# Attention times values with the values stationary: two 64-column halves of the array, one head in each

## The chip, the cores and the metric

The kernel runs on one core of one Trainium2 chip. The metric is the device time of one execution in microseconds (us). TensorE (PE) multiplies matrices; its weight loads are listed apart as PEld. VectorE (DVE), ScalarE (ACT) and GpSimd (POOL) work on elements; SyncE (SP) issues most DMAs. Every engine works through its own instructions strictly in the order in which they were written down.

## The reference

One decoder layer over 256 tokens of width 1024. The token mixer has three groups (a gated recurrence, a gated linear attention of 4 heads, and causal softmax attention of 8 heads of width 64), whose outputs go side by side through one output projection; a squared-ReLU MLP follows. With 256 tokens there is one key block, so the attention group is plain causal attention with a linear position bias:

```python
s_own = jnp.einsum('bhqd,bhld->bhql', q_blk, k_own) * scale
s_own = jnp.where(rel >= 0, s_own - slopes[:, None, None] * rel, NEG)
p = jax.nn.softmax(scores, axis=-1)
out = jnp.einsum('bhql,bhld->bhqd', p_own, v_own)
...
y = jnp.concatenate([rms_norm(ya, lru_out_norm), yb, rms_norm(yc, att_out_norm)], axis=-1)
x = x + jnp.einsum('bse,ed->bsd', y, w_out)
```

The attention output `yc` (256 tokens x 512 channels) is normalised over its 512 channels and multiplied by a gain per channel before the output projection.

## The kernel before, in words

Large products run as three matmuls (`mm3`, L299): every float32 operand is split into a high part of type float32r (an ACT copy, L71) and a low part (a DVE subtraction, L72), and high x high, high x low and low x high are added up. The small products of the three groups run in plain float32; the trace shows each of these matmuls as two records, one for each pass, so `x4` stands for two matmuls (a transpose has one record).

Weights come in chunks of 128x2048; chunk 0 to 11 are the input projection, 12 to 15 the output projection (two rows of 128 channels each), the rest is the MLP. `split_w` (in the plan `S_`, L96) splits half a chunk, and the second half also issues the load of the chunk three further on.

PE's order is written out: `slots` (L821) is the list of the quarters of the input projection (slots 8 to 47: twelve matmuls of 256 columns each), then the output projection (from slot 48: one channel block `k`, one quarter of the output, three matmuls of 512 columns each). Slots 48 to 63 take channel blocks 0 to 3, slots 64 to 67 channel blocks 4 to 7 of the first output quarter, and so on. The table `plan` (L826) names the steps that are issued ahead of each slot. A step puts its instructions into the queues of whichever engines it uses. So the table sets the order on all engines.

Of attention, each head `h` goes through: `at_mm` (scores for two heads; the two heads stand on different 64-row halves of the array, and each writes a PSUM bank of its own, L641), `at_max` (DVE, L646), `at_exp` (ACT with row sums, L653 and L654), `at_tr` (three PE transposes of the 128x384 probabilities, L659), `at_pt` (ACT copies the result to SBUF, L663). Then for four heads at a time: `at_av` multiplies with the values. There the transposed probabilities are stationary (128 columns to load) and 64 value columns stream (L674 to L676), so the output has tokens on partitions. `at_norm` (DVE, L683 and L684) divides by the row sums, `at_sq` (ACT, L691) makes sums of squares, `at_rms` and `at_scale` (DVE and POOL, L696, L152, L701) apply the norm per token. `at_out_tr` transposes the result with eight PE transposes (L168), since the output projection wants channels on partitions, and `at_out_split` (L175, L176) applies the gain and splits into `yTh` and `yTl`.

PSUM has eight banks; `mis` takes the one that has been idle longest, `free` gives it back.

Of the kernel before, what the change touches and what calls it, by code (L numbers as in the profile page):

```python
# [11 lines left out]
AF = mybir.ActivationFunctionType  # L12
OP = mybir.AluOpType
AX = mybir.AxisListType

P = 128
# [12 lines left out]
SP_LAM, SP_LB, SP_LN, SP_AN, SP_WA, SP_WX, SP_N = 30, 32, 34, 36, 40, 296, 552  # L29
# [3 lines left out]
def trunk_kernel(ctx: ExitStack, tc, x, x_t, w_in, w_out, w_ff1, w_ff2, small, hg_norm, norm_final, out):  # L33
    nc = tc.nc
    V, A, G, T = nc.vector, nc.scalar, nc.gpsimd, nc.tensor
# [12 lines left out]
    def mis(name):  # L48
        b = idle.pop(0)
        held[name] = (b,)  # L50
        return banks[:, b, :]
# [55 lines left out]
    sp = xa[:, 0:SP_WA]  # L107
# [33 lines left out]
    ident = const.tile([P, P], F32, name="ident")  # L141
# [23 lines left out]
    def transposes(pair, src, k0, t):  # L165
        for n in range(4):
            i = n // 2
            T.transpose(pair[n % 2][:, i * 256 + t * 128:i * 256 + (t + 1) * 128],  # L168
                        src[:, t, (k0 + n) * P:(k0 + n + 1) * P], ident)

    def evac_split(pair, gain, oh, ol, k0, ns=range(4)):
        for n in ns:
            k = k0 + n
            ps = pair[n % 2][:, (n // 2) * 256:(n // 2 + 1) * 256]
            A.activation(oh[:, k, :], ps, AF.Copy, scale=gain[:, k:k + 1])  # L175
            V.scalar_tensor_tensor(ol[:, k, :], ps, gain[:, k:k + 1],  # L176
                                   oh[:, k, :].bitcast(F32), op0=OP.mult, op1=OP.subtract)

    ones = const.tile([P, 64], F32, name="ones")
# [150 lines left out]
    yTh = wt("yTh", [P, KT, S], dt=F32R)  # L330
    yTl = wt("yTl", [P, KT, S], dt=F32R)
# [7 lines left out]
    att_d = wt("att_d", [P, 8, 128])  # L339
# [126 lines left out]
    rr = {}  # L466
# [33 lines left out]
    su = wt("su", [P, 512])  # L500
# [111 lines left out]
    cq = [wt(f"cq{g}", [P, 2, 256], tag=("cq0", "xb_y")[g]) for g in range(2)]  # L612
    ck = [wt(f"ck{g}", [P, 2, 256]) for g in range(2)]
    cv = wt("cv", [P, 2, 512])
    oc = wt("oc", [P, 2, 512])
    rsum = wt("rsum", [P, 2, 8])
    ps_s, sc_t, nm_t, pr_t, ps_t, PT = {}, {}, {}, {}, {}, {}

# [42 lines left out]
    def at_pt(h):  # L661
        PT[h] = wt("PT", [P, 384], tag="PT", bufs=8)
        A.copy(PT[h], ps_t[h][:, 0:384])  # L663
        free(f"pt{h}")

    ps_o = {}

    def at_av(g):
        ps = ps_o[g] = mis(f"av{g}")
        o = ps.rearrange("p (t h e) -> p t h e", t=2, h=4)  # L670
        for r in range(4):
            h = 4 * g + r
            vs = slice(h * 64, h * 64 + 64)
            T.matmul(o[:, 0, r, :], PT[h][:, 0:128], cv[:, 0, vs], start=True, stop=True)  # L674
            T.matmul(o[:, 1, r, :], PT[h][:, 128:256], cv[:, 0, vs], start=True, stop=False)  # L675
            T.matmul(o[:, 1, r, :], PT[h][:, 256:384], cv[:, 1, vs], start=False, stop=True)  # L676

    css = wt("css", [P, 2, 2])
    csq = wt("csq", [P, 2, 256], tag="su")

    def at_norm(g):
        ri = wt("ri", [P, 2, 4], tag="ri", bufs=2)
        V.reciprocal(ri, rsum[:, :, 4 * g:4 * g + 4])  # L683
        V.tensor_tensor(oc[:, :, g * 256:(g + 1) * 256].rearrange("p t (h e) -> p t h e", e=64),  # L684
                        ps_o[g].rearrange("p (t h e) -> p t h e", t=2, h=4),
                        ri[:, :, :, None].to_broadcast([P, 2, 4, 64]), op=OP.mult)
        free(f"av{g}")

    def at_sq(g):
        for t in range(2):  # L690
            A.activation(csq[:, t, :], oc[:, t, g * 256:(g + 1) * 256], AF.Square,  # L691
                         accum_out=css[:, g, t:t + 1])

    def at_rms():
        c2 = wt("c2", [P, 2])
        V.tensor_tensor(c2, css[:, 0, :], css[:, 1, :], op=OP.add)  # L696
        rr["c"] = rms_scale(c2, 512, 2, "cr")

    def at_scale():
        for t in range(2):  # L700
            V.tensor_scalar(oc[:, t, :], oc[:, t, :], rr["c"][:, t:t + 1], None, op0=OP.mult)  # L701

    oT = {}

    def at_out_tr():
        oT[0] = [mis(f"oT{b}") for b in range(2)]
        for t in range(2):
            transposes(oT[0], oc, 0, t)

    def at_out_split():  # L710
        evac_split(oT[0], sp[:, SP_AN:SP_AN + 4], yTh[:, 4:8, :], yTl[:, 4:8, :], 0)
        free("oT0")
        free("oT1")


    tn = [(0, 0), (1, 0), (0, 1), (1, 1)]
# [95 lines left out]
    def x1_ss():  # L812
        for t in range(2):
# [6 lines left out]
    S_ = split_w  # L820
# [39 lines left out]
        33: [(hg_pred, 16), (at_mm, 0), (hg_mm, 32)],  # L860
        34: [(lr_ss,), (at_max, 0), (S_, 10, 1), (hg_pred, 32), (at_q, 1)],
        35: [(hg_up, 32)],
        36: [(lr_rms,), (at_max, 1), (at_exp, 0), (S_, 12, 0), (at_tr, 0), (at_k, 1)],
        37: [(hg_mm, 64), (at_mm, 1), (lr_bc,), (lr_rl,)],
        38: [
            (at_max, 2), (at_bias, 3), (at_pt, 0), (hg_pred, 64), (hg_up, 64), (at_exp, 1), (at_mm, 2),
            (at_bias, 4), (at_max, 3), (at_tr, 1), (at_max, 4), (lr_norm,), (hg_mm, 128), (at_exp, 2),
        ],
        39: [(at_bias, 5), (at_exp, 3), (at_tr, 2), (at_pt, 1), (at_max, 5), (S_, 11, 0)],
        40: [(at_mm, 3), (at_bias, 6), (hg_cross,), (hg_v,), (at_exp, 4), (at_max, 6)],  # L870
        41: [(at_bias, 7), (hg_av,), (at_tr, 3), (at_tr, 4), (at_max, 7)],
        42: [(at_pt, 2), (at_pt, 3), (S_, 12, 1)],
        43: [(at_exp, 5), (at_exp, 6), (S_, 11, 1), (hg_sq,), (hg_rms,)],
        44: [(at_pt, 4), (at_tr, 5), (at_v, 0), (S_, 13, 0), (at_exp, 7)],
        46: [(at_av, 0), (at_tr, 7), (at_norm, 0), (hg_out,), (at_pt, 7)],
        47: [(at_tr, 6), (at_pt, 5), (at_sq, 0)],
        48: [(x_load,), (lr_split,), (at_pt, 6)],
        50: [(hg_tr,), (S_, 13, 1)],
        51: [(at_v, 1), (at_av, 1), (at_norm, 1), (at_sq, 1)],
        52: [(at_rms,), (hg_split,)],  # L880
        54: [(at_scale,)],
        55: [(S_, 14, 0)],
        57: [(at_out_tr,)],
        58: [(S_, 14, 1)],
        63: [(S_, 15, 0), (at_out_split,)],
        64: [(S_, 15, 1), (S_, 16, 0)],
        68: [(S_, 16, 1)],
        72: [(x1_add, 0, 0), (x1_add, 1, 0)],
        77: [(x1_tr, 0, 0), (x1_tr, 0, 1)],
# [173 lines left out]
```

## Time and profile before

| what | value |
|---|---|
| median of 3 runs | 318.41 us (317.84 to 319.43) |
| profiled execution | 317.64 us, of which span 315.9 us |
| granted TensorE clock | 0.997 of full |
| PE busy | 307.5 us, 97% |
| DVE, ACT, POOL busy | 204.5, 173.6, 36.4 us |

The span runs from the first to the last instruction; 1.74 us of the profiled execution lie outside it. Matmuls are pipelined, so the duration of one record is longer than the time that it takes from its engine. The chain of waits cuts the span into pieces that follow one another; where PE is never idle, a piece of that chain is what an instruction costs PE.

### The profile page before, as it was taken

How to read it: one execution, taken by the hardware profiler on the slowest of the kernel's cores; microseconds unless marked ns; L12 is line 12 of the kernel's file. 1: busy time of each engine (PE TensorE's matmuls, PEld its weight loads, DVE VectorE, ACT ScalarE, POOL GpSimd, SP SyncE). 2: the span in 40 equal slices, each digit the busy share in tenths (PEclk: the TensorE clock that was granted, in tenths of full speed). 3: DMA queues.
4: the chain of work that ended last, by engine and by line, in shares of the span. 5: the costliest groups of instructions: out<-in, count | busy, mean ns of one | idle time of the engine just before them, and what ended most of it. 6: DMA issues, size and time to landing. Idle time of an engine off the chain costs nothing.

```text
span 315.9 us, 4816 instructions
## 1 busy us (share of the span) xinstructions
PE 307.5 (97%) x1908; PEld 270.7 (86%) x1908; DVE 204.5 (65%) x317; ACT 173.6 (55%) x297; POOL 36.4 (12%) x83
## 2 busy tenths in 40 slices
PE   8999999999999999999999999999999999999991
PEld 7999999998999888888888888888888888888881
DVE  1848999984545494686867745845754674575573
ACT  4769699684585370676635633552662463355241
POOL 8338900021401000000000000000000000000000
PEclk9999999999999999999999999999999999999998
DMA  7996553361036337038674366257336536621003
GB/s 198 411 399 231 189 214 133 135 226 41 2 135 266 134 134 268 0 133 334 261 270 166 110 257 228 92 214 264 118 151 266 164 114 256 233 102 65 0 9 126
DMA packets 9959, 55.68 MB, mean 176 GB/s; under 512 B 1232, under 2 KB 1488, under 8 KB 4048
## 3 DMA queue, kind: packets, MB, share of 16 engines
q1 hardware_dynamic: 9216, 54.06, 45.9%
q10 hardware_dynamic: 720, 1.31, 1.3%
q8 instruction: 15, 0.25, 0.3%
q14 instruction: 8, 0.07, 0.1%
HBM read 54.32 MB, written 1.05 MB: 175 GB/s over the span
## 4 chain that ended last, share of the span: by engine, by line
PE 93%; DMA 2%; issue 2%; DVE 1%; ACT 1%; POOLq 0%; POOL 0%; ACTq 0%; DVEq 0%
PE banks L770 19%; PE banks L301 19%; PE banks L302 18%; PE banks L303 18%; PE banks L771 10%; PE banks L405 2%; DMA raw<-in_w_in_dram 2%; PE banks L641 1%; PE banks L659 1%; PE banks L168 1%; PE banks L676 1%; PE banks L675 1%; PE banks L458 1%; PE banks L521 1%; PE banks L674 1%
## 5 line engine op out<-in xcount | busy, mean ns | idle before, releaser
L72 DVE TENSOR_TENSOR wl<-raw,wh 128x1024 fp32r<-128x1024 f32 (+1 forms) x100 | 113.6, 1183 | 21.5 <-ACT wh L71 21.5
L71 ACT CAST wh<-raw 128x1024 fp32r<-128x1024 f32 (+1 forms) x100 | 95.5, 1010 | 3.6 <-DMA raw<-in_w_in_dram 3.6
L770 PE MATMUL banks<-x1c,wh 128*128 128x512 f32 x256 | 90.9, 397 | 0.0
L771 PE MATMUL banks<-x1c,wl 128*128 128x256 f32 x256 | 71.8, 281 | 0.0
L770 PEld LDWEIGHTS banks<-x1c,wh 128*128 128x128 f32 x256 | 48.0, 188 | 11.7 <-DVE x1c L176 0.2
L302 PE MATMUL banks<-wl,uh 128*128 128x512 f32 (+1 forms) x132 | 51.4, 389 | 0.0
L303 PE MATMUL banks<-wh,ul 128*128 128x512 f32 (+1 forms) x132 | 51.4, 389 | 0.0
L301 PE MATMUL banks<-wh,uh 128*128 128x512 f32 (+1 forms) x132 | 51.4, 389 | 0.0
L771 PEld LDWEIGHTS banks<-x1c,wl 128*128 128x128 f32 x256 | 48.3, 189 | 0.7
L782 ACT COPY fb<-banks 128x256 f32<-128x256 f32 x32 | 11.8, 371 | 62.5 <-PE banks L771 62.5
L784 DVE TENSOR_TENSOR fs<-banks,fb 128x256 f32<-128x256 f32 x32 | 13.3, 423 | 42.9 <-ACT fb L782 42.9
L301 PE MATMUL banks<-hT,wh 128*128 128x256 f32 x128 | 37.5, 293 | 0.0
L302 PE MATMUL banks<-hT,wh 128*128 128x256 f32 x128 | 36.4, 284 | 0.5 <-DVE hT L162 0.5
L303 PE MATMUL banks<-hT,wl 128*128 128x256 f32 x128 | 36.3, 283 | 0.0
L303 PEld LDWEIGHTS banks<-wh,ul 128*128 128x128 f32 x132 | 24.8, 188 | 5.8 <-DVE ul L788 0.2
L301 PEld LDWEIGHTS banks<-wh,uh 128*128 128x128 f32 x132 | 24.8, 188 | 5.7
L302 PEld LDWEIGHTS banks<-wl,uh 128*128 128x128 f32 x132 | 24.9, 188 | 5.1
L302 PEld LDWEIGHTS banks<-hT,wh 128*128 128x128 f32 x128 | 24.5, 191 | 1.0 <-DVE hT L162 0.9
L301 PEld LDWEIGHTS banks<-hT,wh 128*128 128x128 f32 x128 | 24.6, 192 | 0.5
L303 PEld LDWEIGHTS banks<-hT,wl 128*128 128x128 f32 x128 | 24.5, 191 | 0.1
L969 POOL TENSOR_TENSOR r<-v,nhalf 128x1 f32<-128x1 f32 x2 | 1.1, 550 | 200.3 <-DVE v L965 200.3
L787 ACT CAST uh<-fu 128x512 fp32r<-128x512 f32 x16 | 9.9, 620 | 22.6 <-DVE fu L786 22.6
(197 smaller groups left out, 416.3 us busy)
## 6 DMA issues: line engine op xcount, KB each, us to landing
raw<-in_w_ff_dram SPq DMA_DIRECT2D x32, 1024.0 KB, 4.9
raw<-in_w_in_dram SPq DMA_DIRECT2D x10, 1024.0 KB, 5.9
raw<-in_w_out_dram SPq DMA_DIRECT2D x4, 1024.0 KB, 4.8
raw<-in_w_in_dram ACTq DMA_DIRECT2D x4, 256.0 KB, 7.2
xtok<-in_x_dram SPq DMA_DIRECT2D x2, 512.0 KB, 7.9
xa<-in_x_dram SPq DMA_DIRECT2D x2, 512.0 KB, 6.1
xa<-in_x_t_dram SPq DMA_DIRECT2D x3, 256.0 KB, 6.5
raw<-in_w_in_dram SPq DMA_DIRECT2D x2, 256.0 KB, 8.2
```

What stands on the lines that cost most here:

```text
L71: A.copy(hi, src)
L72: V.tensor_tensor(lo, src, hi.bitcast(F32), op=OP.subtract)
L168: T.transpose(pair[n % 2][:, i * 256 + t * 128:i * 256 + (t + 1) * 128], src[:, t, (k0 + n) * P:(k0 + n + 1) * P], ident)
L301: T.matmul(o, lh, rh, start=first, stop=False)
L302: T.matmul(o, lh, rl, start=False, stop=False)
L303: T.matmul(o, ll, rh, start=False, stop=last)
L405: T.matmul(ps[:, par, g * 64:(g + 1) * 64], kB[r, hp, hs], rhs, start=True, stop=True)
L770: T.matmul(o, wh[:, k, cs], flat(x1c[:, k]), start=k == 0, stop=False)
L771: T.matmul(o[:, 0:S], wl[:, k, cs], x1h[:, k, :], start=False, stop=k == KT - 1)
L782: A.copy(b[:, c, :], ff1_ps[j, c][:, S:])
L784: V.tensor_tensor(s_[:, c, :], ff1_ps[j, c][:, 0:S], b[:, c, :], op=OP.add)
L787: A.copy(uh[j], u)
```

## The change

The product with the values is turned round. The values of a head (64 columns) are stationary, and the transposed probabilities stream (256 columns for the first key block, 128 for the second). Two heads are paired: the output of the even one goes to partitions 0 to 63 of a bank, that of the odd one to partitions 64 to 127 of the same bank. The result has channels on partitions, as the output projection wants it, and the eight transposes of `oc` are gone. Since tokens now lie along the free axis, the division by the row sums is done ahead of the transposes, on the probabilities (`at_nrm`, DVE). The norm over channels is summed by a matmul with ones (`at_ss`), spread to all partitions by a matmul (`at_bc`), and applied together with the gain (`at_y`). The plan table is reordered from slot 36 to slot 68.

```diff
+    def at_nrm(h):
+        ri, pr = wt("ri", [P, 2], tag="ri", bufs=2), pr_t[h]
+        V.reciprocal(ri, rsum[:, :, h])
+        for t, s_ in enumerate((slice(0, 128), slice(128, 384))):
+            V.tensor_scalar(pr[:, s_], pr[:, s_], ri[:, t:t + 1], None, op0=OP.mult)
...
-    def at_av(g):
-        ps = ps_o[g] = mis(f"av{g}")
...
-            T.matmul(o[:, 0, r, :], PT[h][:, 0:128], cv[:, 0, vs], start=True, stop=True)
-            T.matmul(o[:, 1, r, :], PT[h][:, 128:256], cv[:, 0, vs], start=True, stop=False)
-            T.matmul(o[:, 1, r, :], PT[h][:, 256:384], cv[:, 1, vs], start=False, stop=True)
+    def at_av(c):
+        if c % 2 == 0:
+            av = mis(f"av{c // 2}")
+            ps_o[c], ps_o[c + 1] = av[:, 0:256], av[:, 256:512]
+        o = ps_o[c]
+        for kb, qs, ps in ((0, slice(0, 256), slice(0, 256)), (1, slice(128, 256), slice(256, 384))):
+            for par in range(2):
+                h = 2 * c + par
+                T.matmul(o[par * 64:(par + 1) * 64, qs], cv[:, kb, h * 64:(h + 1) * 64], PT[h][:, ps],
+                         start=kb == 0, stop=kb == 1)
...
+    def at_sq(c):
+        A.activation(osq_c[:, c, :], ps_o[c], AF.Square)
+    def at_sum(c, d):
+        V.tensor_tensor(osq_c[:, c, :], osq_c[:, c, :], osq_c[:, d, :], op=OP.add)
+    def at_ss():
+        ps_o["s"] = mis("ass")
         for t in range(2):
+            T.matmul(ps_o["s"][:, t * 64:(t + 1) * 64], osq_c[:, 0, t * 128:(t + 1) * 128], ones,
+                     start=True, stop=True)
     def at_rms():
+        rr["c"] = rms_scale(ps_o["s"].rearrange("p (t e) -> p t e", e=64)[:, 0:2, 0], 512, 2, "cr")
+        free("ass")
+    def at_bc():
+        ps_o["b"] = mis("RCps")
         for t in range(2):
-            V.tensor_scalar(oc[:, t, :], oc[:, t, :], rr["c"][:, t:t + 1], None, op0=OP.mult)
...
-            transposes(oT[0], oc, 0, t)
...
+            T.matmul(ps_o["b"][:, t * 128:(t + 1) * 128], rr["c"][:, t:t + 1].to_broadcast([P, P]), ident,
+                     start=True, stop=True)
+    def at_rl():
+        A.copy(RC, ps_o["b"][:, 0:256])
+        free("RCps")
+    def at_y(c):
+        V.scalar_tensor_tensor(yc[:, c, :], ps_o[c], sp[:, SP_AN + c:SP_AN + c + 1], RC,
+                               op0=OP.mult, op1=OP.mult)
+        if c % 2:
+            free(f"av{c // 2}")
+    def at_split(g):
+        ks = slice(4 + 2 * g, 6 + 2 * g)
+        split(flat(yTh[:, ks, :]), flat(yTl[:, ks, :]), flat(yc[:, 2 * g:2 * g + 2, :]))
...
-        46: [(at_av, 0), (at_tr, 7), (at_norm, 0), (hg_out,), (at_pt, 7)],
+        46: [(at_av, 0), (at_av, 1), (at_tr, 7), (hg_out,), (at_sq, 0), (at_sq, 1), (at_pt, 7)],
```

Three places show what the table moves. On PE, at slot 38, stand the scores of the third pair of heads (L641 before, L640 now), the transposes of head 1 (L659) and a product of the linear attention that also uses 64-row halves (L396). Before and now:

```order
-L641 MATMUL banks<-ck_199,cq_197 128x128 x2
-L641 MATMUL banks<-ck_199,cq_197 128x256 x2
-L659 MATMUL banks<-ident,pr 128x128 x3
+L640 MATMUL banks<-ck_199,cq_197 128x128 x2
+L640 MATMUL banks<-ck_199,cq_197 128x256 x2
 L396 MATMUL banks<-qd,kB 128x128 x4
```

The transposes no longer stand between the two products with 64-row halves; they come one slot later, alone.

On PE, at slot 46, before: the product with the values of heads 0 to 3 (four times three rows), then the transposes of head 7 and slot 46 itself.

```order
L303 MATMUL banks<-wh_1097,hT 128x256
L674 MATMUL banks<-cv,PT 128x64
L675 MATMUL banks<-cv,PT 128x64
L676 MATMUL banks<-cv,PT 128x64
...
L659 MATMUL banks<-ident,pr 128x128 x3
L301 MATMUL banks<-wh_1097,hT 128x256
```

The same place now:

```order
L303 MATMUL banks<-wh_1106,hT 128x256
L681 MATMUL banks<-PT,cv 64x256 x2
L681 MATMUL banks<-PT,cv 64x128 x2
...
L658 MATMUL banks<-ident,pr 128x128 x3
L301 MATMUL banks<-wh_1106,hT 128x256
```

Twelve matmuls of 64 streamed columns became eight matmuls on 64-column halves, four of 256 and four of 128 streamed columns; the second group of heads has the same rows at slot 50.

On DVE, from slot 50 on (`wl_1262` and `wl_1372` are the low parts of the output projection's chunks 13 and 14, `wl_1433` that of chunk 15), now:

```order
L72 TENSOR_TENSOR wl_1262<-raw_945,wh_1261 128x1024
L72 TENSOR_TENSOR wl_1372<-raw_1229,wh_1371 128x1024
L692 TENSOR_TENSOR osq_c<-osq_c 128x256 x2
L72 TENSOR_TENSOR yTl<-banks,yTh 128x512
L72 TENSOR_TENSOR wl_1372<-raw_1229,wh_1371 128x1024
L151 TENSOR_SCALAR crv<-banks 128x2
L715 SCALAR_TENSOR_TENSOR yc<-banks,xa,RC 128x256 x2
L72 TENSOR_TENSOR yTl<-yc,yTh 128x512
L715 SCALAR_TENSOR_TENSOR yc<-banks,xa,RC 128x256 x2
L72 TENSOR_TENSOR yTl<-yc,yTh 128x512
L72 TENSOR_TENSOR wl_1433<-raw_1203,wh_1432 128x1024 x2
```

Both halves of chunk 14 now stand ahead of the norm (`crv`), where before they stood behind it, and the whole tail of attention stands ahead of chunk 15.

## Rows read from the trace of the kernel before

**Rows 1.** The page: busy times, and the chain that ended last by engine.
```profile
PE 307.5 (97%) x1908; PEld 270.7 (86%) x1908; DVE 204.5 (65%) x317; ACT 173.6 (55%) x297; POOL 36.4 (12%) x83
...
PE 93%; DMA 2%; issue 2%; DVE 1%; ACT 1%; POOLq 0%; POOL 0%; ACTq 0%; DVEq 0%
```

**Rows 2.** Waits of PE's weight loads, 60 to 140 us: total, times, longest.
```profile
PEld banks L594 <- issue: 0.3, 1, 0.3
```

**Rows 3.** Busy time by engine in the attention stage (us, then busy and count).
```profile
69.50:101.90 32.40, 32.40 (x286) 30.71 (x285) 15.46 (x43) 19.52 (x57) 7.96 (x7) 1.00 0.33 127
```

**Rows 4.** Chain of waits, 94 to 113 us: start, length (us), what.
```profile
95.74 0.17 PE banks L674 x2
...
98.36 0.33 PE banks L659 x3
...
104.42 0.17 PE banks L674 x2
...
107.05 0.28 PE banks L301
107.33 0.23 PE banks L302
...
111.21 0.87 PE banks L168 x8
```

**Rows 5.** Chain of waits, 73 to 84 us.
```profile
74.31 0.71 PE banks L641 x8
...
77.94 0.48 PE banks L659 x3
...
80.69 0.33 PE banks L659 x3
...
82.45 0.86 PE banks L641 x8
83.31 0.31 PE banks L301
83.62 0.12 PE banks L302
```

**Rows 6.** Chain of waits, 67 to 69 us.
```profile
68.18 0.39 PE banks L584 x4
68.58 0.17 PE banks L301
```

**Rows 7.** Chain of waits, 21.5 to 24 us.
```profile
22.41 0.45 PE banks L232 x4
```

**Rows 8.** Chain of waits, 44 to 49 us.
```profile
45.09 0.86 PE banks L521 x4
```

**Rows 9.** The page's costliest groups: a weight load of the input projection.
```profile
L302 PEld LDWEIGHTS banks<-hT,wh 128*128 128x128 f32 x128 | 24.5, 191 | 1.0 <-DVE hT L162 0.9
```

**Rows 10.** DVE by line and shape, 75 to 116 us (busy, mean ns).
```profile
L72 DVE TENSOR_TENSOR wl<-raw,wh 128x1024 fp32r<-128x1024 f32 x8 | 9.6, 1223 | 5.8 <-ACT wh L71 5.8
...
L701 DVE TENSOR_SCALAR oc<-oc,crr 128x512 f32<-128x512 f32 x2 | 0.9, 485 | 0.0
L605 DVE SCALAR_TENSOR_TENSOR ya<-ya,xa,RL 128x256 f32<-128x256 f32 x2 | 0.9, 478 | 0.0
...
L151 DVE TENSOR_SCALAR crv<-c 128x2 f32<-128x2 f32 x1 | 0.2, 169 | 0.0
```

**Rows 11.** ACT by line and shape, 75 to 116 us.
```profile
L71 ACT CAST wh<-raw 128x1024 fp32r<-128x1024 f32 x9 | 9.2, 1049 | 0.0
...
L691 ACT ACTIVATE csq<-oc 128x256 f32<-128x256 f32 x4 | 1.6, 416 | 4.9 <-DVE oc L684 4.9
...
L71 ACT CAST yTh<-banks 128x512 fp32r<-128x512 f32 x1 | 0.6, 566 | 0.0
```

**Rows 12.** POOL by line and shape, 60 to 116 us.
```profile
L152 POOL TENSOR_TENSOR hrr<-hrv,nhalf 128x8 f32<-128x8 f32 x1 | 1.7, 1665 | 8.7 <-DVE hrv L151 8.7
...
L152 POOL TENSOR_TENSOR crr<-crv,nhalf 128x2 f32<-128x2 f32 x1 | 0.7, 697 | 13.4 <-DVE crv L151 13.4
```

More of the change, by code (lines that the diff above doesn't have):

```diff
@@ L614, in trunk_kernel @@
     cv = wt("cv", [P, 2, 512])
-    oc = wt("oc", [P, 2, 512])
     rsum = wt("rsum", [P, 2, 8])
@@ L664, in at_pt @@
         free(f"pt{h}")
-    ps_o = {}
-    def at_av(g):
-        ps = ps_o[g] = mis(f"av{g}")
[L670 to L673, printed above, removed]
-            T.matmul(o[:, 0, r, :], PT[h][:, 0:128], cv[:, 0, vs], start=True, stop=True)
-            T.matmul(o[:, 1, r, :], PT[h][:, 128:256], cv[:, 0, vs], start=True, stop=False)
-            T.matmul(o[:, 1, r, :], PT[h][:, 256:384], cv[:, 1, vs], start=False, stop=True)
@@ L678, in trunk_kernel @@
[L678 to L689, printed above, removed]
+    def at_nrm(h):
[3 more added lines that the diff above has]
+            V.tensor_scalar(pr[:, s_], pr[:, s_], ri[:, t:t + 1], None, op0=OP.mult)
@@ L690, in at_sq @@
+    osq_c = wt("osq_c", [P, 4, 256], tag="oc")
+    yc = wt("yc", [P, 4, 256], tag="att_d")
+    RC = wt("RC", [P, 256], tag="su")
+    def at_sq(c):
[4 more added lines that the diff above has]
+        ps_o["s"] = mis("ass")
         for t in range(2):
-            A.activation(csq[:, t, :], oc[:, t, g * 256:(g + 1) * 256], AF.Square,
-                         accum_out=css[:, g, t:t + 1])
+            T.matmul(ps_o["s"][:, t * 64:(t + 1) * 64], osq_c[:, 0, t * 128:(t + 1) * 128], ones,
+                     start=True, stop=True)
@@ L694, in at_rms @@
     def at_rms():
[L695 to L699, printed above, removed]
+        rr["c"] = rms_scale(ps_o["s"].rearrange("p (t e) -> p t e", e=64)[:, 0:2, 0], 512, 2, "cr")
+        free("ass")
+    def at_bc():
+        ps_o["b"] = mis("RCps")
         for t in range(2):
-            V.tensor_scalar(oc[:, t, :], oc[:, t, :], rr["c"][:, t:t + 1], None, op0=OP.mult)
[L703 to L707, printed above, removed]
-            transposes(oT[0], oc, 0, t)
@@ L710, in at_out_split @@
[L710 to L713, printed above, removed]
+            T.matmul(ps_o["b"][:, t * 128:(t + 1) * 128], rr["c"][:, t:t + 1].to_broadcast([P, P]), ident,
[8 more added lines that the diff above has]
+            free(f"av{c // 2}")
@@ L862, in trunk_kernel @@
         35: [(hg_up, 32)],
-        36: [(lr_rms,), (at_max, 1), (at_exp, 0), (S_, 12, 0), (at_tr, 0), (at_k, 1)],
-        37: [(hg_mm, 64), (at_mm, 1), (lr_bc,), (lr_rl,)],
+        36: [(lr_rms,), (at_max, 1), (at_exp, 0), (S_, 12, 0), (at_k, 1)],
+        37: [(hg_mm, 64), (at_mm, 1), (lr_bc,), (lr_rl,), (at_nrm, 0), (at_tr, 0)],
         38: [
             (at_max, 2), (at_bias, 3), (at_pt, 0), (hg_pred, 64), (hg_up, 64), (at_exp, 1), (at_mm, 2),
-            (at_bias, 4), (at_max, 3), (at_tr, 1), (at_max, 4), (lr_norm,), (hg_mm, 128), (at_exp, 2),
+            (at_bias, 4), (at_max, 3), (at_nrm, 1), (at_max, 4), (lr_norm,), (hg_mm, 128), (at_exp, 2),
@@ L868, in trunk_kernel @@
         ],
[L869 to L874, printed above, removed]
-        46: [(at_av, 0), (at_tr, 7), (at_norm, 0), (hg_out,), (at_pt, 7)],
@@ L876, in trunk_kernel @@
[L876 to L886, printed above, removed]
+        39: [(at_bias, 5), (at_tr, 1), (at_exp, 3), (at_pt, 1), (at_max, 5), (at_nrm, 2), (S_, 11, 0)],
@@ new lines, in trunk_kernel @@
+        40: [(at_mm, 3), (at_tr, 2), (at_bias, 6), (hg_cross,), (hg_v,), (at_exp, 4), (at_nrm, 3), (at_max, 6)],
+        41: [(at_bias, 7), (hg_av,), (at_tr, 3), (at_nrm, 4), (at_max, 7), (lr_split,)],
+        42: [(at_tr, 4), (at_pt, 2), (at_pt, 3), (S_, 12, 1)],
+        43: [(at_exp, 5), (at_exp, 6), (at_nrm, 5), (S_, 11, 1), (hg_sq,), (at_nrm, 6), (hg_rms,)],
+        44: [(at_pt, 4), (at_tr, 5), (at_v, 0), (S_, 13, 0), (at_exp, 7), (at_nrm, 7)],
+        46: [(at_av, 0), (at_av, 1), (at_tr, 7), (hg_out,), (at_sq, 0), (at_sq, 1), (at_pt, 7)],
@@ new lines, in trunk_kernel @@
+        47: [(at_tr, 6), (at_pt, 5), (at_sum, 0, 1)],
+        48: [(x_load,), (at_pt, 6), (at_v, 1)],
+        50: [
+            (hg_tr,), (at_av, 2), (at_av, 3), (S_, 13, 1), (S_, 14, 0), (at_sq, 2), (at_sum, 0, 2), (at_sq, 3),
+            (at_sum, 0, 3),
+        ],
+        52: [(hg_split,), (S_, 14, 1)],
+        53: [(at_ss,), (at_rms,)],
+        56: [(at_bc,), (at_rl,), (at_y, 0), (at_y, 1), (at_split, 0), (at_y, 2), (at_y, 3), (at_split, 1)],
+        60: [(S_, 15, 0), (S_, 15, 1)],
@@ L887, in trunk_kernel @@
+        64: [(S_, 16, 0)],
         68: [(S_, 16, 1)],
```

## The prediction

> **What bounds the kernel now.** Read the busy times first: PE is busy for 97% of the span, DVE for 65%, ACT for 55%; the chain of waits is PE for 93% [rows 1]. A busy PE may still hide idling, so look at what PE waits for next: between 60 and 140 us its weight loads wait five times, none longer than 0.3 us, and matmuls not at all [rows 2]. So in the stage that the change touches time is PE's own instructions, one after the other, and a change is worth what it takes from or adds to them, plus any wait that it opens. DVE and ACT are not the bound there: from 69.5 to 101.9 us DVE is busy for 15.5 of 32.4 us and ACT for 19.5 [rows 3]. As PE is never idle, what an instruction costs is read from the chain's pieces, which follow one another without overlap; the durations of single records do overlap and must not be added.
>
> **Removed from PE.** The product with the values of heads 0 to 3 takes from 95.74 to 98.36, 2.62 us; that of heads 4 to 7 from 104.42 to 107.05, 2.63 us, and the matmul behind it takes 0.28 instead of 0.23, which is 0.05 more [rows 4]. The eight transposes of `oc` take 0.87 us [rows 4]. Together 2.62 + 2.68 + 0.87 = 6.17 us.
>
> **Added on PE.** Each new product for a pair of heads is two matmuls of 256 columns and two of 128 in plain float32, on two halves of the array. No row shows column halves. The nearest are the scores of a pair of heads, `at_mm`: the same four sizes, on two row halves. After matmuls on the whole array they take 0.86 us, and the first whole-array matmul behind them 0.31 instead of 0.12; after another product on row halves they take 0.71 [rows 5]. The same two matmuls on the whole array cost far more: two of 256 columns took 0.86 [rows 8], two of 128 took 0.45 [rows 7], together 1.31. So row halves do run side by side, and changing the shape of the array costs about 0.15 going in and 0.19 going out. If column halves behave like row halves, a block of two pairs costs 0.86 + 0.71 + 0.19 = 1.76 us, and the two blocks 3.52. If the halves run one after the other, the stream alone is 8 x 0.43 + 8 x 0.225 = 5.24, with the changes of shape 2 x 0.34 more: 5.92. I take 3.52, the row of the same sizes, and keep 5.92 as the other end.
>
> The sum over channels by ones (`at_ss`) has its twin in L584, 0.39 us and 0.05 on the matmul behind it [rows 6]; the spreading (`at_bc`) in L232, 0.45 us [rows 7]. Together 0.89.
>
> **Moved on PE.** The transposes of head 1 stood between two products on row halves, and took 0.48 us there, against 0.33 elsewhere [rows 5]. Now the second of these products follows the first, which saves its entry too (0.86 against 0.71). I book 0.15 + 0.15 = 0.30 us saved; the bounds are 0 and 0.34.
>
> Sum on PE: -6.17 + 3.52 + 0.89 - 0.30 = -2.06 us.
>
> **Off PE.** DVE loses `at_norm`, `at_scale` and four gain passes, and gains per head a reciprocal and two scalings. A scaling of 512 columns takes 0.485 and a tiny one 0.17 [rows 10], so those of 128 and 256 lie between, and the three together between 0.5 and 1.14; I take 0.75, 6 us for eight heads. DVE has 17 idle us in that stage, so this costs nothing by its volume. It does stand in a chain: `at_exp`, then `at_nrm`, then `at_tr`, behind which all of PE queues. For heads 0, 1, 2 and 4 the table puts the transposes one slot or a few later, a slot being twelve matmuls at 0.12, 1.44 us, more than the 0.75; for the others at least a slot lies between exponential and transposes already. Cost 0; if a `DVE` split of 1.2 us [rows 10] comes in between, some tenths.
>
> The tail is tighter. Take the end of the input projection (slot 48) as zero. PE: two slots of three 0.23 matmuls, 1.38; the transposes of the linear attention, 0.44; the second block, 1.76; three slots, 2.07: `at_ss` is due at 5.6, and after 0.44 and three more slots `at_bc` at 8.1. On the other side ACT starts the two value copies, then the high parts of chunk 13's second and chunk 14's first half (1.05 each [rows 11]), squares the new product when it ends at 3.6 + 0.4 for the pipeline, done by about 4.4; DVE has done both low parts by 4.2, adds two sums, done at 5.1: `at_ss` doesn't wait, by 0.5. Then come `hg_split` (0.57 and 0.69) and the second half of chunk 14, whose low part on DVE ends at about 7.0, and only behind it the first step of `at_rms` (0.17); POOL's power takes 0.70 [rows 12]: 7.9. So `at_bc` has 0.2 us to spare. Behind it ACT copies (0.4), then DVE and ACT take turns: two gains (0.48 each [rows 10]), high, low, two gains, high, low: about 4.5 us, done at 13.4. PE needs the first of it at slot 64, 8.1 + 0.5 + 8 x 0.69 = 14.1. Then chunk 15: high 13.6 and 14.6, low parts 14.8 and 15.9, against PE's second matmul of slots 66 and 67 at 15.7 and 16.4. Everything is on time, by 0.2 to 0.9 us. Such sums are not good to better than 0.3, so I book 0.25 us of waits; ends 0 and 1.0.
>
> Net -2.06 + 0.25 = -1.8 us. The profiled execution took 317.64 us (315.9 us of span and 1.74 around it), so its like would take 315.8. The median shown, 318.41, is 0.77 above the profiled execution; the saving is the same, and the forecast is 318.41 - 1.8 = 316.6 us.
>
> **Two rules that speak against it.** Whole-array loads do overlap: loads of 191 ns [rows 9] stand in a stream with a matmul every 0.12 us [rows 5]. The Trainium skill (TensorE: Matmul & The Clock Gate, Part 3, "What overlaps and what doesn't") says that a weight load overlaps matmuls in flight only when its row group differs; two column halves share their rows. The row above contradicts the strict form, and by the rule the result would be the first rival's 318.1.
>
> The scores of a pair of heads go to two PSUM banks, and the new pair to one; no row shows two halves writing one bank. The Trainium skill (TensorEngine Tiling, Gotcha 1) says that different row tiles cannot access the same PSUM bank simultaneously; it says so of row tiles, and if it held for column tiles the result would be the second rival's 318.8.
>
> **Rivals.** *Loads in the open.* Each of the 32 loads of 64 columns stands ahead of its matmul. A product with the values takes 0.22 for two loads of 128 columns [rows 4], so 0.056 for one of 64: 32 x 0.056 = 1.8 on top of -2.06, with the tail's waits gone since PE is later: -0.3, 318.1 us. For it: nothing shown; against it: the loads of row halves and of the whole array are hidden.
>
> *One after the other.* 5.92 instead of 3.52: -2.06 + 2.40 = +0.3, 318.8 us. For it: the shared bank, and that two streams of 128 partitions must be read at once where row halves read 64 each. Against it: a plain float32 stream takes about 0.21 us for 256 columns and pass, twice the 0.12 of float32r, so two of them ask for no more reading than one float32r stream.
>
> *Every change of half drains the array*, as a change of shape does: on top of one after the other, seven changes in each block at 0.15: 14 x 0.15 = 2.1, so +2.4, 320.8 us. It decides for slower once a change costs over (1.6 - 0.3) / 14 = 0.09 us. For it: entry and exit do cost 0.15 and 0.19. Against it: `at_mm` also alternates halves, and pays only at its ends.
>
> *The tail is late.* POOL's power took 1.67 us for eight columns and 0.70 for two [rows 12]; if it, or DVE ahead of it, is 1 us later, `at_bc` and what follows hold PE by about 1 us more: -0.8, 317.6 us.
>
> **How the numbers follow.** Forecast 0.66, loads in the open 0.10, one after the other 0.12, drains 0.07, tail late 0.05. Within the forecast's own case the unknown terms leave -2.4 to -1.2, so 316.0 to 317.2, and a median of three runs is itself uncertain by some tenths. A measurement here can tell about 0.5%, 1.6 us, from no change, so the forecast lies just beyond: about two thirds of its 0.66 are faster by more, 0.45; the rest, with loads, one after the other and the late tail, is no change, 0.43; slower is drains with part of one after the other, 0.12. The range reaches from 315.3, the best case less 0.7 for the runs' own spread, to 319.2, which takes in one after the other and leaves out the drains.
>
> **What the profile after would show.** Records of the new product (L681) in pairs a few ns apart, a block of 16 records at about 1.57 us in the chain of waits; single records 0.2 us apart would be the second rival. No wait of PE's at the transposes of a head; at most some tenths ahead of `at_bc` (L707) or ahead of the low-part matmul of slot 67. The spans of all later stages unchanged in length. The forecast is wrong if the two blocks together cost PE more than 4.5 us or if new waits add up to over 1 us.

## The result, and the profile after

The median is 315.75 us (315.17 to 316.03, 4 runs) against 318.35 (317.84 to 319.43) before: ratio 0.9918 [0.9905, 0.9932], 2.6 us faster. The forecast was 316.6, 1.8 faster, with 315.3 to 319.2 as its range. The profiled execution took 316.03 us, span 314.2.

The page's busy times and its chain by engine, against [rows 1]:

```profile
PE 305.0 (97%) x1892; PEld 267.5 (85%) x1892; DVE 210.0 (67%) x339; ACT 173.6 (55%) x292; POOL 35.5 (11%) x83
...
PE 82%; DMA 6%; DVE 5%; ACT 3%; issue 2%; SPq 0%; POOLq 0%; POOL 0%; DVEq 0%
```

PE is still the bound at 97% and lost 2.5 us of busy time; DVE gained 5.5. PE's share of the chain fell from 93 to 82%, and all of that fall lies in the part that wasn't edited. At 41.9 us, between slots 20 and 22, PE waited 0.5 us for a tile of the linear attention from DVE, and from there the chain goes back over DVE, ACT and two DMAs to the start (start, length in us, what):

```profile
14.70 9.02 DMA raw<-in_w_in_dram
...
41.51 0.35 DVE kB L432
...
41.90 1.20 PE banks L405 x16
```

From there to 300 us, through every stage that the change touches, the chain is PE alone. Such a share tells which piece came last, not how much there is to gain: half a microsecond of waiting moved some 33 us of the chain from PE to others.

The chain of the kernel after, the stretch that answers to [rows 4] and [rows 5]:

```profile
75.05 0.71 PE banks L640 x8
...
78.15 0.86 PE banks L640 x8
79.01 0.45 PE banks L396 x8
...
82.83 0.86 PE banks L640 x8
83.69 0.48 PE banks L658 x3
...
96.37 1.45 PE banks L681 x16
97.82 0.48 PE banks L658 x3
...
99.73 0.33 PE banks L658 x3
...
103.33 1.45 PE banks L681 x16
104.78 0.43 PE banks L301
105.21 0.23 PE banks L302
...
107.04 0.39 PE banks L697 x4
107.44 0.29 PE banks L301
...
109.57 0.45 PE banks L707 x4
110.01 0.23 PE banks L301
...
117.75 0.30 PE banks L302
```

A block of two pairs of heads (L681) takes 1.45 us. The transposes behind the first take 0.48 instead of 0.33, the matmul behind the second 0.43 instead of 0.23: leaving the halves costs 0.15 and 0.20. So the two blocks cost 1.60 + 1.65 = 3.25 us, where 3.52 was forecast. `at_ss` (L697) costs 0.39 + 0.06 and `at_bc` (L707) 0.45, together 0.90, where 0.89 was forecast. The scores of the third pair of heads at slot 38 (78.15) are followed directly by another product on row halves, which takes 0.45. Before, with transposes in between, that product took 0.65:

```profile
78.41 0.65 PE banks L396 x8
```

Waits of PE's weight loads, 50 to 140 us (total, times, longest), against [rows 2]:

```profile
PEld banks L594 <- issue: 0.3, 1, 0.3
PEld banks L658 <- issue: 0.3, 1, 0.3
PEld banks L302 <- DVE wl L72: 0.2, 1, 0.2
PEld banks L779 <- DVE x1c L176: 0.2, 1, 0.2
PEld banks L658 <- DVE pr L669: 0.2, 1, 0.2
PEld banks L301 <- issue: 0.2, 1, 0.2
PEld banks L681 <- issue: 0.2, 1, 0.2
```

Among the new waits is one for the scaled probabilities (L669) and one for the low part of a chunk (L72); both hold a weight load for 0.2 us. The first stands at the exit from the first block; at the exit from the second, ahead of L301, a load is held as long with nothing to wait for, so it may cost nothing of its own. Matmuls themselves wait nowhere in this stretch. The load that waits for L72 stands ahead of the matmul at 117.75 in the chain, the only one of the output projection behind slot 56 that takes longer than its like without a transpose or `at_bc` ahead of it, 0.30 instead of 0.23: 0.07 us lost, in slot 67, where the forecast put the danger.

Where the time went, by stages: lengths in us, from the matmuls at the start of one stage to those of the next (the MLP's to the start of its last matmul), worked out from the records of the profiled executions.

| stage | before | after | difference |
|---|---|---|---|
| first matmul to end of slot 35 | 69.65 | 70.72 | +1.07 |
| slot 36 to the output projection | 30.63 | 29.17 | -1.46 |
| output projection | 27.21 | 26.33 | -0.88 |
| MLP | 180.28 | 179.86 | -0.42 |

The first row is the same program in both kernels. In the thirteen traces of this study it lies anywhere from 69.65 to 70.72, so it is a spread between executions. Of the 1.07 us here, 0.45 arise in slots 0 to 2, while the first weights arrive, and 0.61 between slots 20 and 22, with the wait for DVE named above. For this reason the two spans differ by only 1.7 us where the medians differ by 2.6. Without it the trace gives -1.46 - 0.88 - 0.42 = -2.76. The changed stages give -2.34, and 0.42 come from the MLP, whose program wasn't touched.

### The profile page after: what moved, and what is told of

Its sections match the earlier page's. It is cut to its first block, busy times and chain, and to the rows that moved or that the text cites. A ratio compares the mean times of both kernels' runs of the same rounds, so it can differ in the third digit from the quotient of the medians.

```text
span 314.2 us, 4805 instructions
## 1 busy us (share of the span) xinstructions
PE 305.0 (97%) x1892; PEld 267.5 (85%) x1892; DVE 210.0 (67%) x339; ACT 173.6 (55%) x292; POOL 35.5 (11%) x83
## 4 chain that ended last, share of the span: by engine, by line
PE 82%; DMA 6%; DVE 5%; ACT 3%; issue 2%; SPq 0%; POOLq 0%; POOL 0%; DVEq 0%
PE banks L779 19%; PE banks L301 16%; PE banks L302 15%; PE banks L303 15%; PE banks L780 10%; DMA raw<-in_w_in_dram 6%; DVE wl L72 3%; PE banks L405 2%; ACT wh L71 1%; PE banks L640 1%; PE banks L658 1%; PE banks L681 1%; PE banks L168 1%; PE banks L458 1%; PE banks L521 1%
## 5 line engine op out<-in xcount | busy, mean ns | idle before, releaser
L72 DVE TENSOR_TENSOR wl<-raw,wh 128x1024 fp32r<-128x1024 f32 (+1 forms) x100 | 113.9, 1185 | 23.3 <-ACT wh L71 23.3
L301 PE MATMUL banks<-wh,uh 128*128 128x512 f32 (+1 forms) x132 | 51.1, 387 | 0.0
L301 PE MATMUL banks<-hT,wh 128*128 128x256 f32 x128 | 37.6, 293 | 0.6 <-ACT hT L161 0.6
L301 PEld LDWEIGHTS banks<-wh,uh 128*128 128x128 f32 x132 | 24.9, 188 | 5.5
L301 PEld LDWEIGHTS banks<-hT,wh 128*128 128x128 f32 x128 | 24.5, 192 | 1.2 <-ACT hT L161 0.8
```

Source lines behind the costliest of these rows:

```text
L301: T.matmul(o, lh, rh, start=first, stop=False)
```

## The experiments

Each was timed against the kernel before; where no other is named, the edit is made to the kernel after.

**Do the halves run beside each other only when the program alternates them?** The two heads of a pair one after the other:

```diff
-        for kb, qs, ps in (...):
-            for par in range(2):
+        for par in range(2):
+            for kb, qs, ps in (...):
```

> The changed kernel, with the four matmuls of a pair of heads issued head by head (256 and 128 columns of the even head, then 256 and 128 of the odd one) and not half by half. Theory (the gain is that two column halves of the array run side by side, which needs neighbours on different halves): in the order head by head only the seam between the heads can overlap, so a pair costs between 0.95 and 1.28 us of stream and not 0.64; four pairs add 1.2 to 2.5 us, 317.0 to 318.2 against 315.75. Rival (PE looks far enough ahead to pair them whatever the order): no change, within 0.3 us of the changed kernel. Rival (halves never overlap; the gain came from the other edits): no change either, and the records of a pair already stand apart.

315.55 us, ratio 0.9914 [0.9899, 0.9929]: no change, so the theory (317.0 to 318.2) is refuted and the first rival holds. The records in flight in the first 20 ns of a block (minimum, median and longest in ns, first and last start, forms), first of the kernel after:

```profile
L681 PE MATMUL banks<-PT,cv x2: 430/430/430, 96.3 to 96.3; 128*64 128x256 f32 x2
```

With the heads apart, in the first 20 ns and then in the first 0.47 us:

```profile
L681 PE MATMUL banks<-PT,cv x2: 430/430/430, 96.2 to 96.2; 128*64 128x256 f32 x2
...
L681 PE MATMUL banks<-PT,cv x4: 379/404/430, 96.2 to 96.5; 128*64 128x256 f32 x4
```

And its chain:

```profile
96.30 1.50 PE banks L681 x16
...
103.29 1.50 PE banks L681 x16
```

A block takes 1.50 us, not the 2 and more of halves that wait for each other, and two matmuls are in flight from the start in both, though the program has four records of one head ahead of the other's first. In the order of this program the third and fourth record stream 128 columns; the first four that PE starts all stream 256. So PE doesn't start matmuls on different halves strictly in the order in which they were written, against what the section on the chip says of every engine. How far ahead it takes up such work is bounded only by the next run.

**Is it the halves at all?** Heads 0 and 1 on the lower half, one after the other, then heads 2 and 3 on the upper half. The output's channels come out in another order.

```diff
-        for kb, qs, ps in (...):
-            for par in range(2):
-                T.matmul(o[par * 64:(par + 1) * 64, qs], ...)
+        half = slice((c % 2) * 64, (c % 2) * 64 + 64)
+        for par in range(2):
+            h, o = 2 * c + par, ps_o[c - c % 2 + par]
+            for kb, qs, ps in (...):
+                T.matmul(o[half, qs], ...)
```

> The changed kernel, with the heads of a block placed so that neighbours stand on the same half of the array: heads 0 and 1 one after the other on columns 0 to 63, then heads 2 and 3 on columns 64 to 127 (so for heads 4 to 7). Same matmuls, same number of weight loads; the channels of the attention output come out in another order than the output projection and the gain expect. Theory (what the turned product saves is that two halves run side by side): only the seam between heads 1 and 2 can overlap; a block's stream grows from 1.28 us towards 2.56, so each block takes 2.2 to 2.7 us in the chain of waits instead of 1.45, and the time rises by 1.5 to 2.5 us, to 317.1 to 318.2. Rival (the saving is that a 64-column load is cheaper than a 128-column one, and side by side adds nothing): no change, 315.6.

316.76 us, ratio 0.9957 [0.9943, 0.997]: slower than the kernel after by 1.0 us, less than the theory's 1.5 to 2.5 and not the rival's nothing. The same two views of this kernel, the first 20 ns and the chain:

```profile
L681 PE MATMUL banks<-PT,cv x1: 430/430/430, 95.3 to 95.3; 128*64 128x256 f32 x1
```

```profile
95.41 2.15 PE banks L681 x16
...
103.07 2.15 PE banks L681 x16
```

One matmul instead of two is in flight at the start, and the same sixteen records take 2.15 instead of 1.45 per block: 1.4 us for both, and the two changed stages are 29.87 + 27.06 = 56.93 long against 55.50, 1.4 more.

The edit doesn't put all four heads one after the other, though. Heads 1 and 2 stand on different halves, and the theory was wrong that only the seam between them can overlap. In three stretches of the block 0.70 us apart, the records in flight at the same point are:

```profile
L681 PE MATMUL banks<-PT,cv x2: 379/404/430, 95.3 to 95.6; 128*64 128x256 f32 x2
...
L681 PE MATMUL banks<-PT,cv x4: 379/379/430, 96.0 to 96.3; 128*64 128x256 f32 x4
...
L681 PE MATMUL banks<-PT,cv x2: 379/379/379, 96.7 to 97.0; 128*64 128x256 f32 x2
```

That is head 0 alone, heads 1 and 2 side by side, and head 3 alone, 0.65 to 0.70 each by the starts of the records. So the halves do run side by side, and a pair costs no more than a single head. The 1.4 us are the price of losing half of the overlap. All four heads one after the other would take about 0.15 + 4 x 0.65 = 2.75 per block (an estimate from the 0.65 of a pair and the way in, 0.15), 2.6 us more for both blocks; no run does that. A head alone costs about what it cost before (2.62 / 4 = 0.66), so turning the product round gains nothing on the product itself without the pairing.

It also bounds how far ahead PE reaches: head 2, four records behind head 1, starts beside it, but not beside head 0, eight records ahead. What sets the bound was not tried.

**Are the loads hidden?** The same product in tiles of 64 streamed columns, 48 loads per block instead of 16:

```diff
-        for kb, qs, ps in ((0, slice(0, 256), slice(0, 256)), (1, slice(128, 256), slice(256, 384))):
+        for t, u, kb in ((0, 0, 0), (0, 1, 0), (1, 0, 0), (1, 0, 1), (1, 1, 0), (1, 1, 1)):
+            qs = slice(t * 128 + u * 64, t * 128 + u * 64 + 64)
+            ps = slice((t + kb) * 128 + u * 64, (t + kb) * 128 + u * 64 + 64)
...
-                         start=kb == 0, stop=kb == 1)
+                         start=kb == 0, stop=kb == t)
```

> The changed kernel, with each streamed piece cut to 64 columns: 24 matmuls per block instead of 8, so 48 records and 48 weight loads of 64 columns instead of 16, for the same number of streamed columns. Theory (loads of column halves are hidden behind the stream): the stream is unchanged, a record of 64 columns lasts 0.053 us and a load of 64 columns about 0.056, so at the edge of hiding: 0 to 0.3 us more per block, 315.8 to 316.4. Rival (each load stands in the open, 0.056 us): 32 more loads in each block at 0.056, halved if the loads of the two halves overlap: 1.8 to 3.6 us more, 317.5 to 319.3.

315.38 us, ratio 0.9911 [0.9898, 0.9925]: no slower than the kernel after, which fits the theory's 0 to 0.3 us per block and not the rival's 1.8 to 3.6 us more. Chain of waits of this kernel, then its loads by line (as above):

```profile
95.55 1.55 PE banks L683 x48
...
102.58 1.55 PE banks L683 x48
```

```profile
L683 PEld LDWEIGHTS banks<-PT,cv x96: 132/138/138, 95.5 to 103.9; 128*64 128x64 f32 x96
```

32 more loads of 138 ns each cost 0.10 us per block, 3 ns for one: they are hidden. Together with the pairs in flight this contradicts, for column halves, the rule of the Trainium skill (TensorE: Matmul & The Clock Gate, Part 3, "What overlaps and what doesn't") that a load overlaps matmuls in flight only when its row group differs. The other rule of the Trainium skill (TensorEngine Tiling, Gotcha 1), that different row tiles can't access one PSUM bank at the same time, has no counterpart for column tiles here: both halves write one bank, and go side by side.

**What do the moved transposes buy?** The transposes of heads 0, 1, 2 and 4 straight behind their division, as far forward as they stood before:

```diff
-        36: [..., (S_, 12, 0), (at_k, 1)],
-        37: [(hg_mm, 64), (at_mm, 1), (lr_bc,), (lr_rl,), (at_nrm, 0), (at_tr, 0)],
+        36: [..., (S_, 12, 0), (at_nrm, 0), (at_tr, 0), (at_k, 1)],
+        37: [(hg_mm, 64), (at_mm, 1), (lr_bc,), (lr_rl,)],
...
-            (at_bias, 4), (at_max, 3), (at_nrm, 1), (at_max, 4), ...
-        39: [(at_bias, 5), (at_tr, 1), ..., (at_nrm, 2), (S_, 11, 0)],
+            (at_bias, 4), (at_max, 3), (at_nrm, 1), (at_tr, 1), (at_max, 4), ...
+        39: [(at_bias, 5), ..., (at_nrm, 2), (at_tr, 2), ..., (S_, 11, 0)],
...
-        42: [(at_tr, 4), (at_pt, 2), (at_pt, 3), (S_, 12, 1)],
+        41: [(at_bias, 7), (hg_av,), (at_tr, 3), (at_nrm, 4), (at_tr, 4), (at_max, 7), (lr_split,)],
+        42: [(at_pt, 2), (at_pt, 3), (S_, 12, 1)],
```

> The changed kernel, with the transposes of heads 0, 1, 2 and 4 back at the slots where the kernel before had them, right behind their scaling on DVE. Theory (merging two products on row halves was worth 0.3 us by the forecast and 0.4 by the two traces, and the later slots also cover the scaling): 0.3 to 0.4 us more for the merge, and PE now waits for the scaling at the transposes of heads 0, 1, 2 and 4, about 0.75 us each at most, less what was slack: 0.5 to 2.5 us more, 316.3 to 318.3. Rival (the places of the transposes do not matter, DVE is always early enough): 0.3 us more or less, 315.5 to 316.1.

318.01 us, ratio 0.9988 [0.9979, 0.9997]: nearly all of the gain is gone, as the theory has it. Waits of PE's weight loads, 50 to 140 us:

```profile
PEld banks L658 <- DVE pr L669: 2.3, 3, 1.1
```

Transposes wait for DVE three times, 2.3 us in all, and the stage from slot 36 is 31.65 long instead of 29.17. This edit also undoes the merged products on row halves. The division costs DVE (DVE by line and shape of the kernel after, 70 to 116 us: busy, mean ns)

```profile
L669 DVE TENSOR_SCALAR pr<-pr,ri 128x256 f32<-128x256 f32 x8 | 3.0, 381 | 0.0
L669 DVE TENSOR_SCALAR pr<-pr,ri 128x128 f32<-128x128 f32 x8 | 2.5, 313 | 1.0 <-DVE ri L667 0.5
...
L667 DVE RECIPROCAL ri<-rsum 128x2 f32<-128x2 f32 x8 | 1.3, 160 | 0.9 <-ACT pr L653 0.9
```

which is 0.381 + 0.313 + 0.160 = 0.85 us per head (0.75 was forecast). It is free only because PE has a slot of 1.44 us of other work in between.

**And the order of the splits in the tail?** The splits of chunks 14 and 15 back behind the norm's steps, about where they stood before, and the recurrence's split (`lr_split`) back from slot 41 to 48:

```diff
-        41: [..., (at_max, 7), (lr_split,)],
+        41: [..., (at_max, 7)],
...
-        48: [(x_load,), (at_pt, 6), (at_v, 1)],
+        48: [(x_load,), (lr_split,), (at_pt, 6), (at_v, 1)],
...
-            (hg_tr,), (at_av, 2), (at_av, 3), (S_, 13, 1), (S_, 14, 0), (at_sq, 2), ...
+            (hg_tr,), (at_av, 2), (at_av, 3), (S_, 13, 1), (at_sq, 2), ...
...
-        52: [(hg_split,), (S_, 14, 1)],
+        52: [(hg_split,)],
+        55: [(S_, 14, 0)],
+        58: [(S_, 14, 1)],
-        60: [(S_, 15, 0), (S_, 15, 1)],
-        64: [(S_, 16, 0)],
+        63: [(S_, 15, 0)],
+        64: [(S_, 15, 1), (S_, 16, 0)],
```

> The changed kernel, with the weight splits of chunks 14 and 15 and the split of the recurrence's output back at the slots of the kernel before (55, 58, 63, 64 and 48). Theory (the gain is PE's own instructions; the splits lie beside them either way): at_bc gets its norm earlier, since one and a half splits no longer stand ahead of it, but a split of chunk 14 now stands between at_bc and the gains, 1 us; all still ahead of slot 64: within 0.4 us of the changed kernel, 315.4 to 316.2. Rival (the order of the splits is what makes the change pay): PE waits ahead of slots 64 to 67 for 1 us or more, 316.8 and up.

316.86 us, ratio 0.9955 [0.9943, 0.9968]: the theory (315.4 to 316.2) missed, and the rival holds. Waits of PE's weight loads:

```profile
PEld banks L302 <- DVE wl L72: 1.6, 3, 0.6
...
PEld banks L707 <- POOL crr L152: 0.2, 1, 0.2
```

The low parts come late by 1.6 us in three places, all in slots 65 to 67, and the output projection takes 27.55 instead of 26.33. The order of the splits is worth 1.1 us by the medians.

**Is the pairing of pairs into blocks worth anything?** Each pair in a block of its own, with whole-array work in between:

```diff
-        46: [(at_av, 0), (at_av, 1), (at_tr, 7), ...
+        46: [(at_av, 0), (at_tr, 7), (at_av, 1), ...
...
-            (hg_tr,), (at_av, 2), (at_av, 3), ...
+            (at_av, 2), (hg_tr,), (at_av, 3), ...
```

> The changed kernel, with whole-array transposes put between the two pairs of each block (those of head 7 in the first, those of the linear attention in the second), so the array changes its shape four times more. Theory (each way in and out costs 0.15 to 0.2 us): 2 x 0.34 = 0.7 us more, 316.3. Rival (the changes of shape are hidden behind other records): no change.

316.6 us, ratio 0.9954 [0.994, 0.9968]. Of the 1.3 us that the trace is longer from slot 36 on, one wait for a head's division is 0.6, so this run gives no clean price for a change of shape. Its chain gives what a block is made of:

```profile
97.64 0.80 PE banks L681 x8
```

One pair takes 0.80, two take 1.45: a pair is 0.65, and going in 0.15.

**All four pairs in one block**, at slot 50, with the transposes of head 7 one slot later, the sums ahead of chunk 14's splits and `at_bc` one slot later:

```diff
-        46: [(at_av, 0), (at_av, 1), (at_tr, 7), (hg_out,), (at_sq, 0), (at_sq, 1), (at_pt, 7)],
-        47: [(at_tr, 6), (at_pt, 5), (at_sum, 0, 1)],
+        46: [(hg_out,)],
+        47: [(at_tr, 6), (at_tr, 7), (at_pt, 5), (at_pt, 7)],
...
-            (hg_tr,), (at_av, 2), (at_av, 3), (S_, 13, 1), (S_, 14, 0), (at_sq, 2), ...
+            (hg_tr,), (at_av, 0), (at_av, 1), (at_av, 2), (at_av, 3), (S_, 13, 1), (at_sq, 0), (at_sq, 1),
+            (at_sum, 0, 1), (at_sq, 2), (at_sum, 0, 2), (at_sq, 3), (at_sum, 0, 3), (hg_split,),
...
-        52: [(hg_split,), (S_, 14, 1)],
+        52: [(S_, 14, 0)],
...
-        56: [(at_bc,), ...
+        54: [(S_, 14, 1)],
+        57: [(at_bc,), ...
```

> The changed kernel, with all four pairs of heads multiplied in one block at slot 50 instead of two blocks at slots 46 and 50; the transposes of head 7 one slot later, the splits of chunk 14 behind the sums of squares, at_bc one slot later. Theory (a block pays 0.35 us for changing the shape of the array and back): 0.35 us less on PE, given back in part by the tail, where two more squares and a later at_bc shift the gains by about 0.7 us against slots 64 to 67, which had some tenths to spare: between 0.3 us less and 0.5 us more than the changed kernel, 315.4 to 316.2. Rival (PE never waits in the tail): 0.35 us less, 315.3.

315.7 us, ratio 0.9929 [0.9916, 0.9941]: the same as the kernel after. Its chain, then the waits of its weight loads:

```profile
100.93 2.75 PE banks L681 x32
```

```profile
PEld banks L302 <- DVE wl L72: 1.0, 2, 0.6
```

Four pairs take 2.75 = 0.15 + 4 x 0.65, so the block saves one way in and one exit, 0.15 each, on PE; the low parts of the chunks are then late by 1.0 instead of 0.2. In the trace the two changed stages are even 0.4 us longer than in the kernel after, which the medians don't show. The tail has no slack left for it.

**The division and the moved transposes alone**, in the kernel before. The product with the values stays as it was; `at_norm` only copies:

```diff
+    def at_nrm(h):
+        ...
     def at_norm(g):
-        V.tensor_tensor(oc[...], ps_o[g]..., ri..., op=OP.mult)
+        V.tensor_copy(oc[:, :, g * 256:(g + 1) * 256], ps_o[g].rearrange("p (t e) -> p t e", t=2))
...
-        36: [..., (S_, 12, 0), (at_tr, 0), (at_k, 1)],
-        37: [(hg_mm, 64), (at_mm, 1), (lr_bc,), (lr_rl,)],
+        36: [..., (S_, 12, 0), (at_k, 1)],
+        37: [(hg_mm, 64), (at_mm, 1), (lr_bc,), (lr_rl,), (at_nrm, 0), (at_tr, 0)],
...
```

> The kernel before, with the division by the row sums ahead of the transposes (at_nrm, eight times three DVE instructions) and the transposes at the changed kernel's slots; the product with the values, the norm and the output transposes as before, with a plain copy where the division was. Theory (on PE only the merge of two products on row halves remains, DVE's extra work is hidden): 0.3 to 0.4 us below the kernel before, 317.9 to 318.1. Rival (the rearranged order of the transposes is itself the gain, and the turned product brings little): 1 us or more below the kernel before.

317.24 us, ratio 0.9973 [0.9963, 0.9982]: faster than the theory's 317.9 to 318.1. From slot 36 to the output projection it takes 30.25 instead of 30.63: the merged products on row halves are worth 0.38 (0.30 forecast, 0.34 at most), and no transpose waits. What the theory didn't expect is another 0.48, and it lies, again, in the MLP.

**Where do the MLP's 0.4 us come from?** First, the kernel before once more, unchanged, to see whether one trace's MLP differs from the next:

> The kernel before, for a second profile. After the attention stage the changed kernel ran 0.4 us shorter in its profile, though the MLP is the same in both. Theory (that difference belongs to the one execution profiled): the MLP of this profile lasts as long as in the changed kernel's profile, within 0.1 us. Rival (the changed kernel leaves the MLP a better start): it again lasts 0.3 to 0.5 us longer.

317.76 us, and an MLP of 180.28, the same to 0.01 us. So it isn't scatter: the theory fails and the rival holds. Two things differ in the MLP without any edit there: which PSUM bank each tile gets, and where in SBUF `uh` and `ul`, the MLP's activations, lie. In the kernel before the first of their buffers begins 209984 bytes into each partition, in the kernel after 32 bytes further on (and `fu`, `fb` and `fs` 32 bytes nearer the start), in the run with the division alone 64. Banks and places were each changed alone in the kernel before, the place by a tile of 64 bytes that nothing reads:

```diff
+    def pad():
+        t = wt("pad", [P, 16])
+        G.memset(t, 0.0)
...
-            (at_max, 2), (at_bias, 3), (at_pt, 0), ...
+            (at_max, 2), (at_bias, 3), (pad,), (at_pt, 0), ...
```

> The kernel before, with one small tile of 64 bytes per partition (written once by POOL, never read) allocated ahead of the transposed probabilities, so that the tiles that the MLP uses for its squared activations (uh, ul) move by 64 bytes in SBUF; PSUM banks and all other instructions as before. In the profiles, the MLP of the changed kernel and of the run with the division first was 0.42 and 0.47 us shorter than before, spread evenly over some 900 matmuls, a few ns each. Theory (it is the place in SBUF): the MLP shortens by 0.4 us, 317.8. Rival (it is the PSUM banks, or something else): MLP as before within 0.1 us, 318.2.

```diff
+    def turn():
+        idle.append(idle.pop(0))
...
+        80: [(turn,)],
```

> The kernel before, with the list of idle PSUM banks turned by one ahead of slot 80, so that the MLP's accumulators stand in other banks; SBUF addresses and all other instructions as before. Theory (the shorter MLP comes from SBUF places): MLP as before within 0.1 us, 318.2. Rival (it comes from the banks): the MLP's length changes by 0.2 us or more, in either direction.

The 64 bytes: 317.74 us, ratio 0.999 [0.9981, 0.9999], MLP 179.80. The turned banks: 318.39, ratio 1.0009 [1.0, 1.0018], MLP 180.26. Both theories hold. The matmuls that read `uh` (min, median and longest in ns, first and last start), in the kernel before:

```profile
L301 PE MATMUL banks<-wh,uh x132: 277/396/400, 140.8 to 309.0; 128*128 128x512 f32 x124, 128*128 128x256 f32 x8
```

with the 64 bytes ahead:

```profile
L301 PE MATMUL banks<-wh,uh x132: 279/392/399, 141.1 to 308.7; 128*128 128x512 f32 x124, 128*128 128x256 f32 x8
```

and with the banks turned:

```profile
L301 PE MATMUL banks<-wh,uh x132: 278/396/400, 141.2 to 309.5; 128*128 128x512 f32 x124, 128*128 128x256 f32 x8
```

The median matmul is 4 ns shorter when the tiles begin 64 bytes later, and the stretch 167.6 instead of 168.2 us; this turn of the banks does nothing. In the kernel after the median is 392 too. In all traces the same holds: the three with `uh` and `ul` at the old place have an MLP of 180.26 to 180.28, the ten with them 32 or 64 bytes further on 179.73 to 179.95. So the 0.42 us are most likely a by-product: the new tiles of attention move `uh` and `ul`; the 32 bytes were not tried by themselves. Why the place matters stays open. It isn't only the matmuls that read the moved tiles: by the starts of the records, 0.26 of the 0.48 us lie between matmuls that read `uh` or `ul`, and 0.23 between those that read `x1c`, which stayed where it was. In the kernel after the first kind is 0.71 us shorter and the second 0.32 longer.

## Why the prediction was right, point by point

- **PE is the bound, and a change is worth what it takes from PE.** Held: the changed stages are 2.34 us shorter, and the terms read from the chain add up to that: -6.17 + 3.25 + 0.90 - 0.38 + 0.07 = -2.33.
- **The two blocks, 3.52.** Right in kind (the halves run side by side), 0.27 too dear: 3.25. The scores' 0.86 and 0.71 [rows 5] were taken over for the same sizes; on column halves a pair costs 0.65 instead of 0.71. Going in, 0.15, and the exits, 0.15 and 0.20, were as read.
- **The merged products, -0.30.** Measured alone 0.38, beyond the bound of 0.34: the product behind the scores lost 0.20 of its length, not 0.15.
- **Waits, +0.25.** In the trace 0.07 of them reach a matmul. Their places were right: slot 67's low part, and nothing ahead of `at_bc`, which the forecast had 0.2 us ahead of need.
- **DVE's division costs nothing.** Right, for the reason given: without the later transposes it costs 2.3 us. The tail's "on time by 0.2 to 0.9" was nearly right, and as narrow: one low part came 0.2 us late, with the splits later the run lost 1.1 us, and the 0.30 of the single block were eaten by the same low parts.
- **"The spans of all later stages unchanged in length."** Wrong: the MLP is 0.42 us shorter. It is the one step that failed in kind, since the prediction asked what the change does to instructions and queues, and not to the places of tiles.
- **The rivals.** Loads in the open: 48 loads in place of 16 cost 0.10 us. One after the other: even with half of the overlap taken away the kernel is at 316.76, 1.0 us behind the kernel after; the rival's price, 2.40 for all of it, agrees with the 2.6 estimated from that run. Drains at every change of half: the halves alternate in the kernel after, in a block of 1.45. Tail late: no such wait.

The forecast's 1.8 thus became 2.6 through 0.27 (blocks), 0.08 (merge) and 0.18 (waits), which make the 2.34 of the changed stages, and 0.42 (MLP). That sums to 2.76; the medians show 2.60, and the 0.16 between lie within the runs' spread. The forecast came within 0.9 us with its mechanism intact, but that all four misses point the same way, one of them from a stage that it didn't consider, is chance.

## What to carry to other kernels

Where an output is 64 wide per head, try the narrow operand as the stationary one, two heads on the two column halves: here, in plain float32, the result came out transposed without extra work, and the halves ran side by side without help from the program's order. The gain on the product came from the pairs; count 0.3 us for the way in and out of a block, and leave as few blocks as the rest allows. A step that is added to a dependent chain on another engine is free only with other work of the busy engine in between, so move its consumer along with it, and price the move by undoing it alone. Compare also stages that weren't edited: here one became 0.4 us faster, most likely because tiles moved in memory.

## What the runs showed of the hardware that was not expected

- The two column halves overlap whether or not the program alternates them (1.45 and 1.50 us per block): PE starts a matmul on the other half ahead of three records that were written before it. A pair side by side costs 0.65 us, a head alone 0.65 to 0.70.
- 64 bytes in the place of `uh` and `ul` in SBUF change the MLP by 0.48 us of 180.28, about half of it in matmuls that don't read them.
- The first 70 us of one and the same program vary by up to 1.07 us between profiled executions, so spans alone would have shown 1.7 of the 2.6 us.
